# Side products pinned to their written order in TensorE's queue, and the recurrent norm's transposes written later

## The chip, the cores and the metric

The kernel runs on one core of a Trainium2 chip. The metric is the device time of one execution in microseconds, the median of several runs.

## What is computed

One inference step of a four-layer decoder trunk over 320 tokens: a prompt of 256 and eight samples of eight. Layers 0 and 3 are sliding-window attention, layer 1 a gated convolution, layer 2 a gated linear recurrence (HGRN2). Each layer is a norm, an input projection, the mixer with a gate, an output projection and a residual add. Weights are shared by prompt and samples, everything is in float32. Cut to the recurrent layer, which the second part of the change touches:

```python
def hgrn2_mixer(h, w_in, norm_g, w_out, lb, s0):
    proj = h @ w_in
    q, fl, i, z = jnp.split(proj, [C_F_DIM, 2 * C_F_DIM, 2 * C_F_DIM + C_I_DIM], axis=-1)
    f = lbf + (1.0 - lbf) * jax.nn.sigmoid(fl.astype(jnp.float32))
    ...
    o, s_t = gla_chunked(q, k, v, log_f, s0)      # 16 heads of 128 keys and 128 values
    o = rmsnorm(o, norm_g).reshape(bsz, t, C_I_DIM).astype(h.dtype)
    y = (jax.nn.silu(z) * o) @ w_out
    return y, s_t
```

## The kernel before

**Weight products.** All projections run through one loop, `run_step`: 132 steps in all, each 256 output columns. A step has 16 k tiles (128 input features each), a k tile six products: for each of two column halves, weight high part times input high part (L207), times input low part (L208), weight low part times input high part (L209). The split in a high and a low part is made on ScalarE (L171) and, as L172, on VectorE, or on GpSimd for every fourth piece in the steps of `POOL_STEPS` (68 to 85 among them). The first two steps have a loop of their own (`run_first`, L282 to L284).

**Lanes.** Everything else is written as generators in eight lanes. After each k tile `run_step` calls `L.pump()`, which moves each lane on in a fixed order: `evac`, `att0`, `att1`, `smp`, `gpr`, `s0l`, `gla`, `nrm`. `yield n` says that the lane goes on n k tiles later. So the written order of the program is: six weight products, then what the lanes write, then six more. What TensorE does for the lanes is called side products here: scores (L609 to L614), transposes of probabilities (L652), probabilities times values (L674, L676), the samples' attention (L704 to L773), and in the recurrent layer L1085 to L1232.

**Queues.** The written order isn't the queue order. The program goes through a scheduler (`schedule_with_timeline_sim=True`) that fills each engine's queue by a timeline of its own: the earliest written instruction that this timeline has as ready comes next. An instruction whose inputs it has as late is passed by instructions written later. `tc.keep_in_program_order` (the kernel's `pin`) ties an instruction behind the last one written before it on its engine; it ties nothing behind the instruction itself, and makes no engine wait. On TensorE, `run_first` and the token sums L411 are pinned in the kernel before; all other products are free.

**The recurrent layer.** Steps come in pairs of heads: q, f and i columns, then gate columns of an earlier pair. For each head, `gla` writes transposes (L1085 to L1090), scores (L1121, L1122), a state product (L1132, L1134), the output (L1155 to L1158), and two products for the samples' states (L1173). `inter`, in the lane `s0l`, multiplies the samples' queries with their states (L1206, two pairs of two, four k tiles apart) and gathers the result on VectorE (L1211, L1213). With the output, `gla` adds `norm` to its own lane. `norm` writes the inverse root on VectorE (small operations on 128x3, L361 to L369), scales the output (L1223), and after a `yield 4` writes three transposes (L1232) and the copy L1233 to the buffer `on`. The gate (`z_evac`) reads `on`, and its split L420/L421 makes the input of the output projection.

Of the kernel before, what the change touches and what calls it, by code (L numbers as in the profile page):

```python
# [97 lines left out]

NORM_A = ((0, 0),)

Y = {"spt": 7, "spv": 7, "qk": 5, "pt": 9, "pv": 6}


def trunk_kernel(ctx, tc, ins, outs):
    nc = tc.nc
    T, V, A, G, SP = nc.tensor, nc.vector, nc.scalar, nc.gpsimd, nc.sync

    def pool(name, bufs, **kw):
        return ctx.enter_context(tc.tile_pool(name=name, bufs=bufs, **kw))
# [19 lines left out]
    ones = const.tile([128, 128], F, name="ones")  # L129
    pv = const.tile([128, PV_W], F, name="pv")  # L130
# [5 lines left out]
    acc = const.tile([128, NTOK], F, name="acc")  # L136
# [19 lines left out]
    def w_dma(to):  # L156
        while wstate["dma"] < min(to, npieces):
            i = wstate["dma"]
            t = raw.get([128, 4, 256])
            SP.dma_start(out=t, in_=wsrc[i // 4][i % 4].rearrange("p (k c) -> p k c", k=4))  # L160
            rawt[i] = t
            wstate["dma"] += 1

    def w_split(to, pin=lambda i: i):
        while wstate["split"] < min(to, npieces):
            i = wstate["split"]
            t = rawt.pop(i)
            h = whp.get([128, 4, 256], R)
            l = wlp.get([128, 4, 256], R)
            e = G if i % 4 == 0 and i // 4 in POOL_STEPS else V  # L170
            pin(A.activation(out=h, in_=t, func=ACTF.Copy))  # L171
            pin(e.tensor_tensor(out=l, in0=t, in1=h.bitcast(F), op=ALU.subtract))  # L172
            raw.free()
            wht[i], wlt[i] = h, l
            wstate["split"] += 1
# [3 lines left out]
    def run_step(getx, evac):  # L179

        s = step_no[0]
        step_no[0] += 1
        while not mm.ok(2):
            L.pump()
        ps = [mm.get([128, NTOK]) for _ in range(2)]
        final = s == len(wsrc) - 1

        def order(k):

            if final and k >= 12:  # L190
                return [(kk, k // 2 - 6) for kk in range(12 + 2 * (k % 2), 14 + 2 * (k % 2))] if k < 16 else []
            return [(k, 0), (k, 1)]

        for k in range(16):
            i = 4 * s + k // 4
            if k % 4 == 0:
                w_dma(i + 4)
                w_split(i + 3)
                w_dma(i + 7)
            while getx(k) is None:  # L200
                L.pump()
            wh, wl = wht[i], wlt[i]
            for kk, o in order(k):
                a = wh[:, kk % 4, o * 128:(o + 1) * 128]
                b = wl[:, kk % 4, o * 128:(o + 1) * 128]
                xh, xl = getx(kk)
                T.matmul(out=ps[o], lhsT=a, rhs=xh, start=(kk == 0), stop=False)  # L207
                T.matmul(out=ps[o], lhsT=a, rhs=xl, start=False, stop=False)  # L208
                T.matmul(out=ps[o], lhsT=b, rhs=xh, start=False, stop=(kk == 15))  # L209
            if k % 4 == 3:  # L210
                whp.free()
                wlp.free()
                del wht[i], wlt[i]
            L.pump()
        L.add("evac", evac(ps))

    def pin(ins):

        return tc.keep_in_program_order(ins)
# [3 lines left out]
    def run_first():  # L223

        ps = [[mm.get([128, NTOK]) for _ in range(2)] for _ in range(2)]
# [48 lines left out]
        def products(k, steps=(0, 1)):  # L274
            for s in steps:
                for o in range(2):
                    c = slice(o * 128, (o + 1) * 128)
                    if s == 0:
                        a, b = (t[:, k % 4, c] for t in wt[0, k // 4])
                    else:  # L280
                        a, b = (t[:, k % 2, c] for t in wt[1, k // 4, k % 4 // 2])
                    pin(T.matmul(out=ps[s][o], lhsT=a, rhs=hH[k], start=(k == 0), stop=False))  # L282
                    pin(T.matmul(out=ps[s][o], lhsT=a, rhs=hL[k], start=False, stop=False))
                    pin(T.matmul(out=ps[s][o], lhsT=b, rhs=hH[k], start=False, stop=(k == 15)))  # L284
                if s == 0 and k % 4 == 3:
                    whp.free()
                    wlp.free()
                if s == 1 and k % 2:
                    dyn.free(2)
# [24 lines left out]
        for k in range(16):  # L314

            if k % 2 == 0 and k < 14:
                j = k + 2
                split(0, j // 4, j % 4, j % 4 + 2)
                tile_h(j)
                split(1, j // 4, j % 4, j % 4 + 2)  # L320
                tile_h(j + 1)
                if j % 4 == 2 and j < 8:
                    load(0, j // 4 + 2, 0, 4)
                    load(1, j // 4 + 2, 0, 4)
                squares(k // 2)
            if k < 14:
                products(k)
        SP.dma_start(out=scv, in_=ins["scv"])

        products(14, (0,))  # L330
        products(15, (0,))
        step_no[0] = 2
        wstate["dma"] = wstate["split"] = 8
# [21 lines left out]
    def wait(p, n=1):  # L355
        while not p.ok(n):
            yield 1

    def rsqrt(x, out, t, scratch_engine=None):

        V.tensor_scalar(out=out.bitcast(I32), in0=x.bitcast(I32), scalar1=1, scalar2=None,  # L361
                        op0=ALU.arith_shift_right)
        V.tensor_scalar(out=out.bitcast(I32), in0=out.bitcast(I32), scalar1=-1, scalar2=0x5F3759DF,
                        op0=ALU.mult, op1=ALU.add)
        V.tensor_scalar(out=x, in0=x, scalar1=-0.5, scalar2=None, op0=ALU.mult)
        for _ in range(3):
            V.tensor_tensor(out=t, in0=out, in1=out, op=ALU.mult)  # L367
            V.tensor_tensor(out=t, in0=t, in1=x, op=ALU.mult)
            V.scalar_tensor_tensor(out=out, in0=t, scalar=1.5, in1=out, op0=ALU.add, op1=ALU.mult)  # L369

    hH, hL = {}, {}
# [33 lines left out]
    def r_job(ticks=3):  # L405
        yield ticks
        yield from wait(sm)
        yield from wait(wk, 2)
        ps = sm.get([128, NTOK])

        pin(T.matmul(out=ps, lhsT=ones, rhs=acc, start=True, stop=True))  # L411
        ms, t = wk.get([128, NTOK]), wk.get([128, NTOK])
        V.tensor_scalar(out=ms, in0=ps, scalar1=1.0 / D, scalar2=EPS, op0=ALU.mult, op1=ALU.add)
        sm.free()
        rsqrt(ms, rb, t)
        wk.free(2)
# [69 lines left out]
    def layer_a(li):  # L486
# [108 lines left out]
        def att_unit(pr, gp, qd, ql):  # L595
            while not (kdone[0] and vdone[0]):
                yield 1
            yield Y["qk"]
            P = {}
# [41 lines left out]
            dyn.free(3)  # L641
            yield Y["pt"]
            parts = {}
            for kv in range(2):
# [3 lines left out]
                for o in range(2):  # L648
# [13 lines left out]
                    yield 1  # L662
            yield Y["pv"]
            yield from wait(xo)
# [23 lines left out]
        def smp_job(pr):  # L688
            while not (kdone[0] and vdone[0]):
                yield 1  # L690
            for hb in range(2):
# [22 lines left out]
                for b2 in range(2):  # L714
# [34 lines left out]
                    tiny.free(3)  # L749
                    yield Y["spt"]  # L750
                    while not (sm.ok(2) and wk.ok(3)):
# [15 lines left out]
                    sm.free(2)  # L767
                    yield Y["spv"]
                    yield from wait(sm)
# [49 lines left out]
        if li == 0:  # L819
            L.add("evac", k_evac(first[0]))  # L820
            L.add("evac", v_evac(first[1]))
        else:
            run_step(get_h, k_evac)
            run_step(get_h, v_evac)
        for pr in range(2):
            for gp in range(4):
                run_step(get_h, q_evac(pr, gp))
# [102 lines left out]
    def layer_c(li):  # L930
# [287 lines left out]
        def norm(h, o, ss):  # L1218
            r, t = tiny.get([128, 3]), tiny.get([128, 3])
            V.tensor_scalar(out=ss, in0=ss, scalar1=1.0 / 128, scalar2=EPS, op0=ALU.mult, op1=ALU.add)  # L1220
            rsqrt(ss, r, t)
            for i in range(3):
                V.tensor_scalar(out=o[:, i, :], in0=o[:, i, :], scalar1=r[:, i:i + 1], scalar2=None, op0=ALU.mult)  # L1223
            tiny.free(3)
            yield 4
            yield from wait(sm)
            if h % 2 == 0:
                yield from wait(xo)
                on[h // 2] = xo.get([128, 2, NTOK])
            pt = sm.get([128, 384])  # L1230
            for i in range(3):
                T.transpose(out=pt[:, i * 128:(i + 1) * 128], in_=o[:, i, :], identity=ident)  # L1232
            A.activation(out=on[h // 2][:, h % 2, :], in_=pt[:, 0:NTOK], func=ACTF.Copy)  # L1233
            sm.free()
            wk.free()
            done.add(h)
# [56 lines left out]
    ps = [sm.get([128, 1]) for _ in sizes]  # L1293
# [7 lines left out]
    for i, (c, n) in enumerate(sizes):  # L1301
        T.matmul(out=pr[:, c:c + n], lhsT=r[0:n, i:i + 1].to_broadcast([n, 128]), rhs=ident[0:n, 0:n], start=True,
                 stop=True)
    for p in range(8):
        for o in (0, 1) if p == 0 else (slice(0, 2),):
            o = slice(o, o + 1) if p == 0 else o
# [133 lines left out]
```

## Time and profile before

| | |
|---|---|
| time, median of 3 runs (lowest, highest) | 2092.29 us (2089.16, 2093.36) |
| profiled execution: time, span | 2096.16 us, 2094.3 us |
| mean granted TensorE clock in it | 0.991 |
| TensorE, VectorE, ScalarE, GpSimd busy | 98%, 68%, 48%, 31% of the span |

The span is that of the profiled execution, from its first to its last instruction; its time has some 2 us around it. Busy time of TensorE is time in which at least one product is under way; products overlap, so the mean time of one is longer than the distance between two starts. The clock is the share of full speed that was granted to TensorE.

### The profile page before, as it was taken

How to read it: one execution, taken by the hardware profiler on the slowest of the kernel's cores; microseconds unless marked ns; L12 is line 12 of the kernel's file. 1: busy time of each engine (PE TensorE's matmuls, PEld its weight loads, DVE VectorE, ACT ScalarE, POOL GpSimd, SP SyncE). 2: the span in 40 equal slices, each digit the busy share in tenths (PEclk: the TensorE clock that was granted, in tenths of full speed). 3: DMA queues.
4: the chain of work that ended last, by engine and by line, in shares of the span. 5: the costliest groups of instructions: out<-in, count | busy, mean ns of one | idle time of the engine just before them, and what ended most of it. 6: DMA issues, size and time to landing. Idle time of an engine off the chain costs nothing.

```text
span 2094.3 us, 36939 instructions
## 1 busy us (share of the span) xinstructions
PE 2051.8 (98%) x13994; PEld 2034.8 (97%) x13994; DVE 1421.2 (68%) x2748; ACT 1008.9 (48%) x2027; POOL 655.1 (31%) x1002
## 2 busy tenths in 40 slices
PE   8989999999999999999999999999999999999997
PEld 8989999999999999999998999999999999999997
DVE  7888865564455455455777998888875677876644
ACT  6567753433333333344454544454544357775442
POOL 0576400110000000012555565345401146752010
PEclk9999999999999999999999999999999999999998
DMA  6433565444444444455454454444465544445542
GB/s 240 129 121 121 181 187 173 151 151 151 150 147 149 150 151 151 154 169 170 145 163 137 161 164 143 163 154 153 145 222 175 170 148 142 127 137 174 166 151 101
DMA packets 106442, 326.45 MB, mean 156 GB/s; under 512 B 16600, under 2 KB 25304, under 8 KB 106264
## 3 DMA queue, kind: packets, MB, share of 16 engines
q1 hardware_dynamic: 105400, 322.75, 47.8%
q8 instruction: 110, 1.80, 0.4%
q10 hardware_dynamic: 864, 1.34, 0.2%
q14 instruction: 68, 0.56, 0.1%
HBM read 301.88 MB, written 22.17 MB: 155 GB/s over the span
## 4 chain that ended last, share of the span: by engine, by line
PE 86%; DVE 7%; ACT 1%; issue 1%; POOL 1%; DMA 0%; DVEq 0%; POOLq 0%; ACTq 0%
PE mm L208 26%; PE mm L209 26%; PE mm L207 26%; DVE wlp L172 1%; PE sm L652 1%; PE sm L674 1%; DVE bg L1176 1%; PE sm L1206 1%; DVE tiny L369 1%; DVE wk L1014 0%; DVE dyn L421 0%; PE sm L1122 0%; PE sm L614 0%; DVE tiny L367 0%; ACT whp L171 0%
## 5 line engine op out<-in xcount | busy, mean ns | idle before, releaser
L207 PE MATMUL mm<-hp,whp 128*128 128x320 f32 x3136 | 976.6, 312 | 2.4 <-DVE wk L428 2.4
L208 PE MATMUL mm<-hp,whp 128*128 128x320 f32 x3136 | 976.5, 311 | 0.0
L209 PE MATMUL mm<-hp,wlp 128*128 128x320 f32 x3136 | 974.3, 311 | 1.2 <-DVE wlp L172 1.2
L171 ACT ACTIVATE whp<-raw 128x1024 fp32r<-128x1024 f32 x520 | 550.4, 1059 | 802.0 <-PE mm L208 660.9
L172 DVE TENSOR_TENSOR wlp<-raw,whp 128x1024 fp32r<-128x1024 f32 x477 | 602.6, 1264 | 466.7 <-ACT whp L171 460.9
L207 PEld LDWEIGHTS mm<-hp,whp 128*128 128x128 f32 x3136 | 590.8, 188 | 4.0 <-DVE wk L428 2.8
L209 PEld LDWEIGHTS mm<-hp,wlp 128*128 128x128 f32 x3136 | 590.4, 188 | 3.5 <-DVE wlp L172 2.2
L208 PEld LDWEIGHTS mm<-hp,whp 128*128 128x128 f32 x3136 | 590.8, 188 | 2.3
L208 PE MATMUL mm<-dyn,whp 128*128 128x320 f32 x1024 | 316.5, 309 | 0.0
L207 PE MATMUL mm<-dyn,whp 128*128 128x320 f32 x1024 | 316.4, 309 | 0.0
L209 PE MATMUL mm<-dyn,wlp 128*128 128x320 f32 x1024 | 316.4, 309 | 0.0
L402 POOL TENSOR_TENSOR acc<-acc,wk 128x320 f32<-128x320 f32 x58 | 62.0, 1070 | 446.8 <-ACT wk L401 444.7
L209 PEld LDWEIGHTS mm<-dyn,wlp 128*128 128x128 f32 x1024 | 192.2, 188 | 0.0
L208 PEld LDWEIGHTS mm<-dyn,whp 128*128 128x128 f32 x1024 | 192.2, 188 | 0.0
L207 PEld LDWEIGHTS mm<-dyn,whp 128*128 128x128 f32 x1024 | 192.2, 188 | 0.0
L172 POOL TENSOR_TENSOR wlp<-raw,whp 128x1024 fp32r<-128x1024 f32 x43 | 105.4, 2451 | 139.2 <-ACT whp L171 134.1
L637 POOL TENSOR_SCALAR wk<-wk,tiny 128x256 f32<-128x256 f32 (+1 forms) x96 | 96.9, 1023 | 25.1 <-ACT bg L778 6.9
L885 POOL COPY wk<-wk 128x2 f32<-128x2 f32 x16 | 2.9, 184 | 296.8 <-DVE wk L875 296.8
L626 ACT ACTIVATE wk<-wk,tiny 128x128 f32<-128x128 f32 (+1 forms) x128 | 56.7, 444 | 21.0 <-DVE tiny L620 20.7
L1203 POOL TENSOR_TENSOR dyn<-bg,dyn 128x512 fp32r<-128x512 f32 x32 | 50.8, 1613 | 44.2 <-ACT dyn L1202 44.2
L1112 POOL TENSOR_TENSOR xo<-xo,lcp 128x512 fp32r<-128x512 f32 x32 | 34.2, 1074 | 82.3 <-DVE xo L1105 80.6
L428 DVE TENSOR_TENSOR wk<-mm,rb 128x320 f32<-128x320 f32 x112 | 50.8, 484 | 12.5 <-PE mm L209 11.8
(268 smaller groups left out, 2284.8 us busy)
## 6 DMA issues: line engine op xcount, KB each, us to landing
raw<-in_a_w_in_dram SPq DMA_DIRECT2D x142, 512.0 KB, 3.6
raw<-in_b_w_in_dram SPq DMA_DIRECT2D x128, 512.0 KB, 3.5
raw<-in_c_w_in_dram SPq DMA_DIRECT2D x128, 512.0 KB, 3.5
raw<-in_a_w_out_dram SPq DMA_DIRECT2D x64, 512.0 KB, 3.5
raw<-in_b_w_out_dram SPq DMA_DIRECT2D x32, 512.0 KB, 3.4
raw<-in_c_w_out_dram SPq DMA_DIRECT2D x32, 512.0 KB, 3.5
bg<-in_s_dram SPq DMA_DIRECT2D x16, 512.0 KB, 4.5
out_hgrn_s_dram<-bg SPq DMA_DIRECT2D x16, 512.0 KB, 2.7
```

Of the source, the lines that this page charges most:

```text
L171: pin(A.activation(out=h, in_=t, func=ACTF.Copy))
L172: pin(e.tensor_tensor(out=l, in0=t, in1=h.bitcast(F), op=ALU.subtract))
L207: T.matmul(out=ps[o], lhsT=a, rhs=xh, start=(kk == 0), stop=False)
L208: T.matmul(out=ps[o], lhsT=a, rhs=xl, start=False, stop=False)
L209: T.matmul(out=ps[o], lhsT=b, rhs=xh, start=False, stop=(kk == 15))
L369: V.scalar_tensor_tensor(out=out, in0=t, scalar=1.5, in1=out, op0=ALU.add, op1=ALU.mult)
L402: G.tensor_tensor(out=acc, in0=acc, in1=t, op=ALU.add)
L428: V.tensor_tensor(out=w[o][:, 0:NTOK], in0=ps[o], in1=rb, op=ALU.mult)
L626: A.activation(out=p[:, c], in_=p[:, c], func=ACTF.Exp, scale=-1.0, bias=mx[:, kv, blk:blk + 1], accum_out=sums[:, kv, blk:blk + 1])
L637: G.tensor_scalar(out=p[:, c], in0=p[:, c], scalar1=sums[:, kv, blk:blk + 1], scalar2=None, op0=ALU.mult)
L1112: G.tensor_tensor(out=t, in0=kv[:, u, 1, :].bitcast(F).unsqueeze(1).to_broadcast([128, 4, 128]), in1=umask[:, 4 * u:4 * u + 4].unsqueeze(2 ...
L1203: G.tensor_tensor(out=sl, in0=src, in1=sh.bitcast(F), op=ALU.subtract)
```

## The change

`T`, by which all products were called, becomes a class whose `matmul` and `transpose` pin each product behind what was written before it on TensorE. The weight products of `run_step` are called through `M`, the plain engine, and stay free. The products that were pinned by hand are pinned by the class. In `norm`, the pause before the transposes goes from 4 to 10 k tiles.

```diff
-Y = {"spt": 7, "spv": 7, "qk": 5, "pt": 9, "pv": 6}
+Y = {"spt": 7, "spv": 7, "qk": 5, "pt": 9, "pv": 6, "nrm": 10}
...
-    T, V, A, G, SP = nc.tensor, nc.vector, nc.scalar, nc.gpsimd, nc.sync
+    M, V, A, G, SP = nc.tensor, nc.vector, nc.scalar, nc.gpsimd, nc.sync
+
+    class T:
+        @staticmethod
+        def matmul(**kw):
+            return tc.keep_in_program_order(M.matmul(**kw))
+
+        @staticmethod
+        def transpose(**kw):
+            return tc.keep_in_program_order(M.transpose(**kw))
...
-                T.matmul(out=ps[o], lhsT=a, rhs=xh, start=(kk == 0), stop=False)
+                M.matmul(out=ps[o], lhsT=a, rhs=xh, start=(kk == 0), stop=False)
...
-                    pin(T.matmul(out=ps[s][o], lhsT=a, rhs=hH[k], start=(k == 0), stop=False))
+                    T.matmul(out=ps[s][o], lhsT=a, rhs=hH[k], start=(k == 0), stop=False)
...
-        pin(T.matmul(out=ps, lhsT=ones, rhs=acc, start=True, stop=True))
+        T.matmul(out=ps, lhsT=ones, rhs=acc, start=True, stop=True)
...
             tiny.free(3)
-            yield 4
+            yield Y["nrm"]
             yield from wait(sm)
```

## Rows read from the trace of the kernel before

**Rows 1.** The page's busy time (us, share of the span) of TensorE and VectorE.

```profile
PE 2051.8 (98%) x13994; PEld 2034.8 (97%) x13994; DVE 1421.2 (68%) x2748; ACT 1008.9 (48%) x2027; POOL 655.1 (31%) x1002
```

**Rows 2.** Groups by line, TensorE, 1640 to 1660 us: count | busy us, mean ns.

```profile
L207 PE MATMUL mm<-dyn,whp 128*128 128x320 f32 x46 | 14.2, 309 | 0.0
```

**Rows 3.** Who waited for whom, TensorE: us in total, times, longest.

```profile
PE sm L1232 <- DVE wk L1223: 10.7, 7, 3.7
PE sm L755 <- DVE wk L747: 5.8, 1, 5.8
...
PE sm L609 <- DVE dyn L586: 3.2, 2, 1.8
```

**Rows 4.** Windows: us, busy time and count by engine, then granted TensorE clock (PEclk).

```profile
300.00:400.00 100.00, 100.00 (x684) 100.00 (x683) 59.06 (x75) 42.72 (x61) 9.33 (x9) 1.00 0.53 168
...
71.50:74.90 3.40, 3.40 (x14) 3.21 (x14) 2.49 (x3) 0.11 (x1) 0.54 (x1) 0.50 0.55 171
146.60:153.40 6.80, 5.91 (x22) 5.28 (x23) 5.82 (x16) 3.11 (x8) 4.21 (x8) 0.50 0.01 5
1109.20:1115.90 6.70, 4.59 (x15) 3.75 (x16) 3.81 (x8) 0.44 (x1) 6.62 (x21) 0.50 0.45 146
1259.40:1262.70 3.30, 3.30 (x14) 3.24 (x15) 1.46 (x3) 1.40 (x3) 0.00 (x0) 0.50 0.52 166
```

**Rows 5.** Groups by line, TensorE, from a layer's first product to its L411.

```profile
L207 PE MATMUL mm<-hp,whp 128*128 128x320 f32 x16 | 4.9, 309 | 0.0
```

**Rows 6.** Between L1206's pairs of head 8 (groups), and L1206 of head 10 (timeline).

```profile
L208 PE MATMUL mm<-hp,whp 128*128 128x320 f32 x8 | 2.5, 309 | 0.0
...
1369.01 1.09 PE L1206 MATMUL sm<-dyn,qzs 128*128 128x512 f32 x4
```

**Rows 7.** Timeline, TensorE: start us, us, line, operation.

```profile
71.61 0.74 PE L612 MATMUL sm<-bg,dyn 128*128 128x512 f32 x1
...
74.23 0.31 PE L611 MATMUL sm<-bg,dyn 128*128 128x128 f32 x1
```

**Rows 8.** Groups by line, VectorE and ScalarE, whole span.

```profile
L1176 DVE SCALAR_TENSOR_TENSOR bg<-bg,tiny,sm 128x128 f32<-128x128 f32 x128 | 35.4, 340 | 5.1 <-PE sm L1173 5.0
...
L1233 ACT ACTIVATE xo<-sm 128x320 f32<-128x320 f32 x16 | 6.9, 431 | 23.6 <-PE sm L1232 23.6
```

**Rows 9.** Groups by line, TensorE, L1155 to L1232: head 13, then head 7.

```profile
L207 PE MATMUL mm<-hp,whp 128*128 128x320 f32 x24 | 7.4, 309 | 0.0
...
L207 PE MATMUL mm<-hp,whp 128*128 128x320 f32 x19 | 5.9, 309 | 0.0
```

**Rows 10.** Timeline at head 6, VectorE and GpSimd; groups of VectorE, 1380 to 1420.

```profile
1255.53 2.17 DVE L369 SCALAR_TENSOR_TENSOR tiny<-tiny,tiny 128x3 f32<-128x3 f32 x1
...
1255.28 2.40 POOL L172 TENSOR_TENSOR wlp<-raw,whp 128x1024 fp32r<-128x1024 f32 x1
...
L369 DVE SCALAR_TENSOR_TENSOR tiny<-tiny,tiny 128x3 f32<-128x3 f32 x6 | 0.9, 158 | 0.1
```

**Rows 11.** Timeline, TensorE: L1232 of heads 1, 6 and 10 [idle before].

```profile
1110.99 0.45 PE L1232 MATMUL sm<-ident,wk 128*128 128x128 f32 x1 [3.69 <-DVE wk L1223]
...
1259.39 0.69 PE L1232 MATMUL sm<-ident,wk 128*128 128x128 f32 x2 [2.04 <-DVE wk L1223]
...
1398.78 0.33 PE L1232 MATMUL sm<-ident,wk 128*128 128x128 f32 x1 [0.20 <-DVE wk L1223]
```

**Rows 12.** Timeline at the recurrent layer's end: ScalarE, VectorE, TensorE.

```profile
1552.18 0.44 ACT L1233 ACTIVATE xo<-sm 128x320 f32<-128x320 f32 x1 [1.04 <-PE sm L1232]
...
1555.44 0.89 DVE L421 TENSOR_TENSOR dyn<-wk,dyn 128x320 fp32r<-128x320 f32 x2
...
1561.95 0.31 PE L207 MATMUL mm<-dyn,whp 128*128 128x320 f32 x1
```

**Rows 13.** Timeline at head 12: the norm's L1223 (VectorE) and L1232 (TensorE).

```profile
1464.14 0.68 DVE L1223 TENSOR_SCALAR wk<-wk,tiny 128x128 f32<-128x128 f32 x3
...
1465.16 0.27 PE L1232 MATMUL sm<-ident,wk 128*128 128x128 f32 x1
```

More of the change, by code (lines that the diff above doesn't have):

```diff
@@ L206, in run_step @@
                 xh, xl = getx(kk)
-                T.matmul(out=ps[o], lhsT=a, rhs=xh, start=(kk == 0), stop=False)
-                T.matmul(out=ps[o], lhsT=a, rhs=xl, start=False, stop=False)
-                T.matmul(out=ps[o], lhsT=b, rhs=xh, start=False, stop=(kk == 15))
+                M.matmul(out=ps[o], lhsT=a, rhs=xh, start=(kk == 0), stop=False)
+                M.matmul(out=ps[o], lhsT=a, rhs=xl, start=False, stop=False)
+                M.matmul(out=ps[o], lhsT=b, rhs=xh, start=False, stop=(kk == 15))
             if k % 4 == 3:
@@ L281, in products @@
                         a, b = (t[:, k % 2, c] for t in wt[1, k // 4, k % 4 // 2])
-                    pin(T.matmul(out=ps[s][o], lhsT=a, rhs=hH[k], start=(k == 0), stop=False))
-                    pin(T.matmul(out=ps[s][o], lhsT=a, rhs=hL[k], start=False, stop=False))
-                    pin(T.matmul(out=ps[s][o], lhsT=b, rhs=hH[k], start=False, stop=(k == 15)))
+                    T.matmul(out=ps[s][o], lhsT=a, rhs=hH[k], start=(k == 0), stop=False)
+                    T.matmul(out=ps[s][o], lhsT=a, rhs=hL[k], start=False, stop=False)
+                    T.matmul(out=ps[s][o], lhsT=b, rhs=hH[k], start=False, stop=(k == 15))
                 if s == 0 and k % 4 == 3:
```

## The prediction

> **What bounds the kernel now.** I read the busy shares of the page first: TensorE is busy for 98% of the span, VectorE for 68% [rows 1]. The kernel therefore ends when TensorE's queue ends, and only two things shorten it: less work in that queue, or less waiting. Then the groups by line for TensorE. Nearly all of it is the 12480 weight products; in a stretch that holds nothing else, 46 of each of their three lines, 138 in all, pass in 20 us, so one takes about 145 ns from start to start, and a k tile of six of them 0.87 us [rows 2]. The change alters neither their number nor their operands, nor those of the side products (transposes, scores, probabilities times values, the recurrence).
>
> What is left is waiting, so the table of TensorE's waits came next [rows 3]. The norm transposes L1232 wait 10.7 us in 7 waits, the sample transposes L755 5.8 us once, the scores L609 3.2 us in two. The other rows are the start, the final norm and a few hand-overs of 1 to 2 us that no edit touches. Last the windows behind the longest waits, for TensorE's clock: behind three of the L1232 waits, behind L755 and behind L609 the granted clock is 0.50, the lower of its two levels, after the engine had stood idle for 1.8 to 5.8 us; in a long stretch without waits it is at the full level [rows 4]. So a wait costs itself and some products at half speed.
>
> What the L1232 waits could give back at most: 10.7 us of idle time, and half of the busy time in the three half-clock windows behind them, 4.59 us at head 1 and 3.30 us at each of heads 6 and 8 (one is shown): 11.19 / 2 = 5.6 us. Together 16.3 us, 0.8% of the time.
>
> **The change, part by part.**
>
> *The pin on side products.* It adds no instruction and no semaphore; it only says that a side product isn't queued ahead of the last TensorE instruction written before it. The weight products lose their only pins in the first two steps to the same class, so those stay pinned, and all later ones stay free. A free weight product written later can therefore still pass a pinned side product whose input is late. The kernel before has such a case: L411, pinned already, is written 24 products into the next layer (three k tiles and the one before its lane is pumped), and in the trace 46 of that layer's products (16 of L207, 15 each of the other two lines) stand ahead of it [rows 5]. So the pin is a floor, not a place, and it moves only those side products that the queue now has ahead of their place, or in another order than two side products were written in.
>
> Ahead of their place: L1206, the state products of the recurrent layer, written in two pairs four k tiles apart. For head 8 the trace has the pairs 24 products apart (8 of each line), as written; for head 10 all four stand in one row [rows 6], and heads 12 and 14 look the same, with one more single product at the layer's start. Those 13 instructions go back by up to 26 products, 26 x 0.145 = 3.8 us later. Bounds: nothing gained, since no idle time is counted before L1206; lost, at most that 3.8 us if its readers had no slack. Their result is first needed by products written eight k tiles on (48 products, 7.0 us), so 3.8 us is hidden by 7.0 us of weight products. I take 0; if that cover were gone, the price is rival 2.
>
> In another order: in the attention layers L612 and L614 of the first key head now run before the second key head's L611 when that one's input is late, as at 71 us: L612 at 71.61, the late L611 at 74.23 [rows 7]. They are written after it, so pinned they wait for it, 2.6 us here; by my count of the queue a dozen of the 32 groups are like this and none moves by more than 70 products (10 us). TensorE loses nothing, as weight products fill in. VectorE gets some score reductions (L620, 0.35 to 0.48 us each) later, but has other work of that layer. In the recurrent layer's first heads two L1173 are likewise held behind late L1157; four L1176 updates of 0.28 us (35.4 / 128) then fall behind the norm instead of ahead of it [rows 8], which could bring L1232 of those two heads forward by 1.1 us each. Bounds for all of this: a gain of 2.2 us, a loss of the same if the order turns the other way. I take 0 to -1 us.
>
> *The transposes, 10 k tiles instead of 4.* What moves is three transposes, the copy L1233 (0.43 us on ScalarE, [rows 8]) and the claim of one output buffer. It issues no DMA, and no DMA queue is passed. The question is whether six k tiles (36 products, 5.2 us) of written place move them in the queue at all. The norm is written together with L1155, so the written place is 24 products behind L1155 before and 60 after. In the trace, head 13 has 70 products between L1155 and its first L1232 (24 of L207, 23 each of the others), head 7 has 56 (19, 19 and 18) [rows 9]; counting all sixteen heads the same way, head 7 is the smallest, thirteen have 69 to 90, and heads 1 and 3, two of those that wait, have 135 and 143. The transposes already stand where the scheduler took the norm to be finished, beyond the new written place in 15 of 16 heads. Moving a floor that lies below them moves nothing; head 7, which has no wait, moves by 4 products (0.6 us). The waits come from elsewhere: the norm's small VectorE operations run later than planned. At head 6 one L369 takes 2.17 us, beside a GpSimd split L172 of 2.40 us that starts at 1255.28 just ahead of it; around head 10, after the last step that gives GpSimd a split, six of them take 0.158 us on average [rows 10]. The transposes then wait 2.04 us [rows 11]. Neither edit changes that meeting, so the waits stay. I take 0 for this edit, with bounds of -16.3 us (above) and +0.6 us.
>
> The Trainium skill ("SBUF — State Buffer", Who interferes with whom) says that a VectorE instruction with two SBUF inputs and a GpSimd instruction that reads SBUF exclude each other for the whole of whichever starts first. The rows of head 6 agree with it. By that rule, heads from 10 on, where no split runs on GpSimd, couldn't get such a wait, and rival 2 would cost nothing; by the rows alone it keeps its price.
>
> What is held longer: the norm's work buffer and the copy's turn on ScalarE, six k tiles in written order. At the layer's end the last head's copy runs at 1552.18, its last split L421 ends at 1556.33, and TensorE first reads it at 1561.95 [rows 12]: 5.6 us of slack against 5.2 us even if the transposes did move by all 36 products. So that end costs nothing either way, but only just.
>
> *Sum.* 0 (L1206) + 0 to -1 (order) + 0 (transposes) = 0 to -1 us. The profiled execution took 2096.16 us (span 2094.3 us), 3.9 us above the median of the runs, 2092.29; I apply the difference to the median: 2091.3 to 2092.3, and forecast 2091.5 us.
>
> **Rivals.**
>
> *1. The written place does decide.* If pinned side products keep their place against later weight products too, the transposes go 36 products (5.2 us) behind, past every late norm: the waits of head 1 (3.69 us) and of heads 6 and 8 (2.04 us) all fit in. All of it gone gives 2092.3 - 16.3 = 2076.0 us. For: six of the seven waits are under 2.1 us. Against: L411 and the counts above.
>
> *2. Later state products make three heads wait (slower).* Heads 6 and 8 have L1206 as written, and their transposes wait 2.04 us; head 10 has L1206 early and waits 0.20 us, heads 12 and 14 don't wait [rows 11]. If the change gives heads 10, 12 and 14 the order of 6 and 8, each costs 2.04 us and half of 3.30 us of work at the lower clock, 3.7 us; three make 11.1 us: 2103.4 us. It decides once the norm ends more than its present lead later: head 12's L1223 ends at 1464.82 and its transpose starts at 1465.16 [rows 13], so 0.3 us is enough there. Against: by the kernel's list of steps, GpSimd takes no split after step 85, and these heads' norms come later.
>
> *3. The first layer's new order takes L755's wait away.* 5.8 us and half of 5.91 us of work at the lower clock [rows 4], 8.8 us: 2083.5 us. For: the wait is one place where VectorE is behind plan, and L612 and L614 are reordered just ahead of it. Against: what VectorE is late by isn't made less by another order, and may only show elsewhere.
>
> **How the numbers follow.** Chances: forecast 0.42 (its own range 2086 to 2098, since a queue that is reordered anywhere shifts waits of 2 us at places nobody names), rival 1 0.25, rival 2 0.23, rival 3 0.10. A change of 0.2%, 4.2 us, is about what a measurement of this kernel tells from none. Faster by more: 0.25 + 0.10 + 0.05 of the forecast's own spread = 0.40; slower by more: 0.23 + 0.05 = 0.28; the rest, 0.32, is within. The range runs from rival 1 to rival 2, 2076 to 2104; full or excess versions of either are left out, some 0.2.
>
> **What the profile after would show.** Right: L1232 of heads 1, 3, 6 and 8 still waits for L1223, about 10 us in all, with 70 and more products between L1155 and L1232; L1206 of heads 10, 12 and 14 in two pairs 24 products apart; L612 never ahead of its group's second L611; half clock behind the same waits. Wrong: no L1232 in TensorE's table of waits (rival 1), L1232 waits of 2 us at heads 10, 12 and 14 (rival 2), no L755 wait near 147 us (rival 3). It would also be wrong if TensorE waited for new releasers in the first layer, through score reductions that come later than VectorE has other work for.

## The result, and the profile after

The changed kernel takes 2080.46 us (median of 4 runs, 2079.55 to 2080.64), the kernel before 2091.91 us in the same comparison: ratio 0.9944, 95% interval 0.9932 to 0.9957. It is 11.4 us faster. The time lies in the range of the prediction, but not at its forecast of 2091.5 us, which was no change.

In the rows of the kernels with pins, pinned products have the line of the class, L113 (matmul) or L117 (transpose), and the tiles tell which they are. Other lines are some 11 or 12 higher than before: the split L172 is L184, the norm's L1223 is L1234, L369 is L381, L620 is L631.

TensorE's waits after (us in total, times, longest), to set beside [rows 3]:

```profile
PE sm L117 <- DVE wk L1234: 5.8, 5, 2.0
...
PE sm L117 <- DVE wk L758: 3.6, 1, 3.6
...
PE sm L113 <- DVE dyn L597: 1.8, 1, 1.8
```

The norm transposes wait 5.8 us where they waited 10.7, the sample transposes 3.6 where they waited 5.8, the scores 1.8 where they waited 3.7 in all (a wait of 1.6 us for a split is new), and the 2.4 us of the last layer's evacuation, too small a row to be among [rows 3], are gone. All rows of that table together make 22.1 us after and 32.4 before: 10.3 us less idle time.

The windows behind the waits (the last numbers are the granted clock, the DMA share and GB/s), beside [rows 4]:

```profile
71.50:74.90 3.40, 3.40 (x24) 3.31 (x25) 3.37 (x6) 0.46 (x2) 0.73 (x2) 1.00 0.52 160
142.80:149.60 6.80, 5.70 (x22) 5.24 (x23) 5.84 (x19) 2.21 (x6) 3.80 (x6) 0.50 0.26 77
1103.00:1109.80 6.80, 6.60 (x44) 6.39 (x45) 3.79 (x7) 3.49 (x5) 4.80 (x5) 1.00 0.41 142
1248.90:1252.20 3.30, 3.30 (x15) 3.30 (x15) 2.93 (x5) 2.27 (x6) 0.00 (x0) 0.50 0.36 118
1317.10:1320.40 3.30, 3.30 (x16) 3.25 (x16) 1.15 (x2) 1.72 (x4) 0.00 (x0) 0.50 0.59 182
```

Of five stretches at the lower level three are left, with 12.3 us of busy time where there were 20.5. Half of the difference is 4.1 us. With the idle time that makes 14.4 of the 15.6 us between the two profiled spans (2094.3 and 2078.7 us). The profiled execution of before was some 4 us above the median of its runs, which is why the medians differ by 11.4 us only.

Not all of the 14.4 us is the change's. e8_pin_l1206 (below) has no pin in the attention layers, and in its trace too the window from 71.50 to 74.90 us is at the full level, with 23 products (14 in the kernel before), and the scores wait 2.4 us. So the gain at the first scores can come without the pins, from one execution to the next.

The parts of the queue that the prediction named: between L1206's pairs of head 10 (groups by line, TensorE, 1357.1 to 1360.5 us; L220 and L221 have 8 each too):

```profile
L219 PE MATMUL mm<-hp,whp 128*128 128x320 f32 x8 | 2.5, 309 | 0.0
```

And head 6's transposes (timeline, TensorE):

```profile
1248.31 1.05 PE L117 MATMUL sm<-ident,wk 128*128 128x128 f32 x5 [1.86 <-DVE wk L1234]
```

L1206 went back to its written place, 24 products apart, as predicted [rows 6]. Head 6's transposes still wait, 1.86 us where it was 2.04 [rows 11], and head 8's 2.03 us; head 1's wait went from 3.69 to 0.86 us.

### The profile page after: what moved, and what is told of

Read it like the earlier page. It is cut to its first block, busy times and chain, and to the rows that moved or that the text cites. A ratio compares the mean times of both kernels' runs of the same rounds, so it can differ in the third digit from the quotient of the medians.

```text
span 2078.7 us, 36968 instructions
## 1 busy us (share of the span) xinstructions
PE 2046.8 (98%) x13994; PEld 2031.6 (98%) x13994; DVE 1406.0 (68%) x2748; ACT 1008.3 (49%) x2027; POOL 669.7 (32%) x1002
## 4 chain that ended last, share of the span: by engine, by line
PE 89%; DVE 6%; POOL 1%; ACT 0%; issue 0%; DVEq 0%; POOLq 0%; ACTq 0%
PE mm L221 27%; PE mm L219 27%; PE mm L220 27%; PE sm L113 6%; PE sm L117 2%; DVE wlp L184 1%; DVE bg L1187 1%; DVE wk L1025 0%; DVE tiny L380 0%; DVE tiny L379 0%; DVE tiny L375 0%; DVE tiny L381 0%; DVE xo L1318 0%; DVE dyn L432 0%; ACT whp L183 0%
## 5 line engine op out<-in xcount | busy, mean ns | idle before, releaser
L221 PE MATMUL mm<-hp,wlp 128*128 128x320 f32 x3136 | 974.1, 311 | 1.6 <-POOL wlp L184 1.6
L220 PE MATMUL mm<-hp,whp 128*128 128x320 f32 x3136 | 974.9, 311 | 0.0
L184 DVE TENSOR_TENSOR wlp<-raw,whp 128x1024 fp32r<-128x1024 f32 x477 | 601.8, 1263 | 473.3 <-ACT whp L183 472.3
L221 PEld LDWEIGHTS mm<-hp,wlp 128*128 128x128 f32 x3136 | 589.6, 188 | 3.1 <-POOL wlp L184 1.8
L220 PEld LDWEIGHTS mm<-hp,whp 128*128 128x128 f32 x3136 | 590.2, 188 | 1.9
L221 PE MATMUL mm<-dyn,wlp 128*128 128x320 f32 x1024 | 316.7, 309 | 0.0
L220 PE MATMUL mm<-dyn,whp 128*128 128x320 f32 x1024 | 316.6, 309 | 0.0
L221 PEld LDWEIGHTS mm<-dyn,wlp 128*128 128x128 f32 x1024 | 192.2, 188 | 0.0
L220 PEld LDWEIGHTS mm<-dyn,whp 128*128 128x128 f32 x1024 | 192.2, 188 | 0.0
L184 POOL TENSOR_TENSOR wlp<-raw,whp 128x1024 fp32r<-128x1024 f32 x43 | 105.5, 2454 | 140.5 <-ACT whp L183 122.7
L648 POOL TENSOR_SCALAR wk<-wk,tiny 128x256 f32<-128x256 f32 (+1 forms) x96 | 104.9, 1106 | 37.0 <-DVE tiny L641 24.8
L117 PE MATMUL sm<-ident,wk 128*128 128x128 f32 (+1 forms) x376 | 65.6, 282 | 9.4 <-DVE wk L1234 5.8
L631 DVE CUSTOM_DVE_ANT_0 wk<-sm,lcp,nsink 128x128 f32<-128x128 f32 (+1 forms) x128 | 46.2, 413 | 22.2 <-PE sm L113 21.9
L117 PEld LDWEIGHTS sm<-ident,wk 128*128 128x128 f32 (+1 forms) x376 | 48.5, 142 | 12.8 <-DVE wk L1234 6.0
```

What stands on the lines that cost most here:

```text
L117: return tc.keep_in_program_order(M.transpose(**kw))
L220: M.matmul(out=ps[o], lhsT=a, rhs=xl, start=False, stop=False)
L221: M.matmul(out=ps[o], lhsT=b, rhs=xh, start=False, stop=(kk == 15))
L631: V.tensor_tensor_reduce(out=p[:, c], in0=S[kv][blk], in1=maskp[:, c], scale=1.0, scalar=nsink[:, 32 * j + h:32 * j + h + 1], op0=ALU.add, ...
L648: G.tensor_scalar(out=p[:, c], in0=p[:, c], scalar1=sums[:, kv, blk:blk + 1], scalar2=None, op0=ALU.mult)
```

## The experiments

Each was compared with the kernel before on the same chip. A ratio is to that kernel.

### The two parts apart: e1_pause, e2_pins

```diff
 e1_pause: kernel before      e2_pins: kernel after
-            yield 4          -..., "nrm": 10}
+            yield 10         +..., "nrm": 4}
```

> The kernel before with the pause of 10 k tiles alone, no product newly pinned. Theory A (the pins reorder the queue and with it VectorE's order; the pause is a floor that lies below the transposes' place): 0, within 4 us of the kernel before, and L1232 still waits some 10 us. Theory B (the written place decides, so the pause makes the gain in the recurrent layer): about 8 us faster, since by the two traces the kernel after gains 8 us of its lead in that layer, and L1232's waits halve.

> The kernel after with the pause put back to 4 k tiles: all pins, no longer pause. Theory A: all of the gain, 11 us faster than before, with L1232 waiting some 6 us as in the kernel after. Theory B: only what the attention layers give, 4 to 7 us faster than before, and L1232 waits 10 us.

The pause alone: 2091.93 us, ratio 1.0003 (0.9995 to 1.0012). The pins alone: 2081.52 us, 0.9954 (0.9941 to 0.9966), against 0.9944 for both. So the pins make nearly all of the gain and the pause alone makes none. Theory A holds for the times. Of the norm transposes' waits in e2_pins it expected 6 us, and they are 8.3 us in 7. With the pins, the pause may give the rest, 1 us, which these intervals don't separate from 0.

```profile
PE sm L1232 <- DVE wk L1223: 9.2, 6, 2.6
```

That is e1_pause's row in the table of waits. It isn't quite as before (10.7 us in 7), and the transposes' places didn't stay: counted in the queue, 12 of 48 stand up to 38 products earlier, and head 7's three stand 4 later, which the prediction had. A changed written order of L1232 and L1233 changes the scheduler's timeline for other operations too.

### Which layer: e3_pins_attn, e4_pins_rec

The pins as in e2_pins, but in one of the two kinds of layer the side products are called through `M`:

```diff
 e3_pins_attn, in layer_c     e4_pins_rec, in layer_a
-T.transpose(...)             -T.matmul(...)
+M.transpose(...)             +M.matmul(...)
```

> The pins on the attention layers' side products alone, pause 4. Both theories: the lead that the kernel after has outside the recurrent layer, 4.5 us in the first layer and 3 us in the last, so 5 to 7.5 us faster than before; the recurrent layer as before, with L1232 waiting some 10 us. If the two attention layers give nothing alone, the gain is all in the recurrent layer and both theories are short.

> The pins on the recurrent layer's side products alone, pause 4. Theory A: 4 to 8 us faster than before, from fewer or shorter L1232 waits at heads 1 to 4, with L755's 5.8 us as before. Theory B: 0, within 4 us, since without the pause the transposes stand where they stood.

The attention layers' pins: 2083.26 us, 0.9965 (0.9953 to 0.9978), 8 us faster. The recurrent layer's: 2088.62 us, 0.9989 (0.9981 to 0.9998), 3 us faster, less than theory A's 4 to 8 and within theory B's 4. The sum is what both give together. The larger part comes from the layers in which the prediction had counted on nothing.

### Which pin in attention: e5_pin_l612, e6_pins_other

```diff
 e5_pin_l612: the only pin on a lane's product but L411; e6_pins_other: this one and the other scores free, the rest of layer_a pinned
-                M.matmul(out=Sb, lhsT=ql[:, o, 128:256], rhs=kb[:, pr, :, :], start=True, stop=False)
+                T.matmul(out=Sb, lhsT=ql[:, o, 128:256], rhs=kb[:, pr, :, :], start=True, stop=False)
```

> Of all pins only the one on the second scores' first product (L612, written behind the second key head's L611) in the attention layers; pause 4. Theory A1 (the gain in attention comes from scores kept in written order, so that all products of a group run together): the same 8 us as with all attention pins, 2083 us, and the L755 wait at 3.6 us. Theory A2 (any other order of the first layer's queue would do as well or as badly: the waits fall where they happen to): a time between 2080 and 2095 us, with waits at other places.

> The pins on all side products of the attention layers but the scores (transposes, probabilities times values, the samples' products); pause 4. Theory A1: no gain, within 4 us of the kernel before, L755 waits 5.8 us as before. Theory A2: again a time between 2080 and 2095 us with waits at other places, a gain as likely as a loss.

One pin, on L612, gives as much as the whole change: 2079.66 us, 0.9948 (0.9935 to 0.9960), more than the 8 us expected. The other attention pins: 2087.89 us, 0.9984 (0.9975 to 0.9993), 2.7 us faster. (The class also pins the first two steps, L411 and the final norm's products in both; e8_pin_l1206 has these pins too and gains nothing.) Two rows of TensorE's timeline in e5_pin_l612, and one of its table of waits, show how:

```profile
72.85 0.22 PE L622 MATMUL sm<-bg,dyn 128*128 128x128 f32 x1
72.91 0.44 PE L113 MATMUL sm<-bg,dyn 128*128 128x512 f32 x1
```

```profile
PE sm L766 <- DVE wk L758: 1.1, 1, 1.1
```

The second scores' first product (L113 here) now stands right behind the second L611 (L622 here); before, it ran 2.6 us ahead of it [rows 7]. The sample transposes wait 1.1 us instead of 5.8. Windows from 60 to 200 us, first of e8_pin_l1206, which has no pin on this layer's products, and then of e5_pin_l612, tell what that is worth:

```profile
60.00:200.00 140.00, 130.78 (x899) 127.49 (x898) 114.84 (x328) 96.74 (x289) 95.28 (x120) 0.98 0.39 129
```

```profile
60.00:200.00 140.00, 135.47 (x944) 132.63 (x943) 117.17 (x345) 102.69 (x310) 101.93 (x123) 1.00 0.42 133
```

TensorE starts 45 products more with the pin, some 6.5 us at 0.145 us each, in single executions. e6_pins_other has 898, so its 2.7 us don't come from here. VectorE's table of waits between 60 and 200 us, first of the kernel before and then of e5_pin_l612, has one row that falls with that wait:

```profile
DVE dyn L658 <- ACT dyn L657: 5.9, 6, 2.1
```

```profile
DVE dyn L669 <- ACT dyn L668: 1.3, 3, 0.5
```

These are the splits of the transposed probabilities. VectorE stood 5.9 us in six waits before them, 1.3 us in three with the pin; e6_pins_other still has 5.9 us, and L755's wait of 5.8. But its waits for the scores (L620 for L611, L631 for L622) grew from 7.4 to 11.3 us, so these rows alone don't explain the sample transposes' shorter wait, and in e3_pins_attn the splits wait 1.3 us too while those transposes wait 3.6. What is shown is the end of it: VectorE comes to L744, from which L747 and then the sample transposes follow, at 146.46 us in the kernel before, at 144.81 in e8_pin_l1206 and at 140.28 in e5_pin_l612. So a TensorE order that costs TensorE nothing brought VectorE's work for the samples forward, and TensorE got the time back some 70 us later, at the sample transposes. By which operations it did so wasn't followed. Theory A2 isn't out by this for the last layer: there the 2.4 us of waits behind the evacuation are gone in e5_pin_l612 and e6_pins_other alike, with different orders.

### Which pin in the recurrent layer: e7_pin_l1173, e8_pin_l1206

```diff
 e7_pin_l1173                                 e8_pin_l1206
-M.matmul(out=sp, lhsT=kv[:, u, 0, :], ...    -M.matmul(out=ps, lhsT=qz[:, u, :], ...
+T.matmul(out=sp, lhsT=kv[:, u, 0, :], ...    +T.matmul(out=ps, lhsT=qz[:, u, :], ...
```

> Only the products L1173 pinned behind the outputs L1157 and L1158; pause 4. The prediction's order term: the four state updates L1176 (0.28 us each) fall behind the norm at heads 1 and 3, whose waits of 3.7 and 1.9 us get shorter by 1.1 us each: 0 to 2.2 us faster than before, most of the 2.8 us that all recurrent pins gave. Rival: the recurrent pins' gain is another pin's (L1121, L1122): no change, waits of 3.7 and 1.9 us as before.

> Only the state products L1206 pinned, so that those of heads 10, 12 and 14 go back to their written place, 26 products later; pause 4. The prediction's sum: 0, within 2 us of the kernel before. Its rival 2: 11 us slower, L1232 waiting 2 us at heads 10, 12 and 14.

L1206 alone: 2092.35 us, 1.0004 (0.9995 to 1.0013). No change, as the sum had it, and no new waits at heads 10 to 14; rival 2 is out. L1173 alone: 2087.55 us, 0.9981 (0.9973 to 0.9990), as much as all pins of that layer and some 3 us where 0 to 2.2 were expected. But not by what I had expected. VectorE's timeline at head 1 in e7_pin_l1173 (the state updates, the norm's first operation, its last):

```profile
1094.90 2.15 DVE L1187 SCALAR_TENSOR_TENSOR bg<-bg,tiny,sm 128x128 f32<-128x128 f32 x8
1096.96 0.16 DVE L1231 TENSOR_SCALAR tiny<-tiny 128x3 f32<-128x3 f32 x1
...
1104.44 0.68 DVE L1234 TENSOR_SCALAR wk<-wk,tiny 128x128 f32<-128x128 f32 x3
```

The eight updates do run later, but still ahead of the norm, not behind it. Other work of VectorE changed places with them, and the norm starts 7.0 us before TensorE reaches the transposes (at 1104.01) where it was 4.5 us in the kernel before (L1220 at 1102.82, TensorE there at 1107.30). Head 1's wait falls from 3.69 to 0.86 us, and head 3's of 1.90 us is gone. Head 4's goes from 0.5 to 0.6 us, and a new one of 1.1 us comes at head 5.

### The written place set behind the norm: e10_pause24, e13_pause24_only

The change with a pause of 24 k tiles, and the kernel before with that pause and no pin.

```diff
 e10_pause24: kernel after     e13_pause24_only: kernel before
-..., "nrm": 10}               -            yield 4
+..., "nrm": 24}               +            yield 24
```

> The kernel after with a pause of 24 k tiles instead of 10, so that the transposes' written place lies behind the place where they stand now (12 of 16 heads stood less than 14 k tiles, 84 products, behind it). Floor theory: now the written place decides, L1232's waits (5.8 us in the kernel after) go below 1 us, and with the half clock behind them 6 to 9 us are gained: 2072 to 2075 us, unless the last heads' output comes too late for the output projection, where 12 us of later transposes stand against 5.6 us of slack: then a new wait of some 5 us there and 2077 to 2080 us. Rival: the waits come from VectorE being late as a whole and only move to other side products: 2080 us as the kernel after.

> The kernel before with a pause of 24 k tiles and no new pin. Floor theory: the written place now lies behind the place where the norm is ready in nearly all heads, so L1232's waits (10.7 us) go below 1 us; as in the run with all pins and this pause, up to 6 us of waits at other side products of heads 1 to 5 take their place: 5 to 10 us faster than before, 2081 to 2086 us, and heads 6 to 10 without any wait. Rival (waits only move): 0.

Without pins: 2080.82 us, 0.9950 (0.9937 to 0.9964), 10 us faster, just under what I expected. With all pins: 2076.69 us, 0.9929 (0.9915 to 0.9942), between the floor theory's 2072 to 2075 and the rival's 2080. L1232 isn't in either table of waits any more. Other products of the first heads wait instead, for VectorE's L1116 (3.0 us in three) and L1224 (1.7 us once) above all in e10_pause24.

In e10_pause24 they make 6 us, about what L1232 waited in the kernel after, and no stretch of the recurrent layer is at the lower clock there. The time is 3.8 us below the kernel after's, but the intervals of the two ratios overlap, so this gain isn't clear of noise. In e13_pause24_only they make 3.9 us against 11.9 us of the kernel before. No wait shows at the layer's end.

### Two splits taken from GpSimd: e12_splits

```diff
-POOL_STEPS = set(range(3, 14)) | set(range(68, 86)) | set(range(108, 122))
+POOL_STEPS = set(range(3, 14)) | set(range(68, 86)) - {81, 85} | set(range(108, 122))
```

> The kernel after with the split L172 (L184 there) of steps 81 and 85 moved from GpSimd to VectorE, the two that stand beside the norm's small operations of heads 6 and 8. Lock theory: L369 (L381 there) beside it takes 0.2 instead of 2.2 us, and the waits of heads 6 and 8 (1.86 and 2.03 us) go below 0.5 us; VectorE pays 1.2 us twice, inside its idle time: 2076 to 2079 us. Rival: VectorE is late by its own 1.2 us in place of the 2 us, waits of about 1 us stay: 2079 to 2081 us.

2072.93 us, 0.9912 (0.9899 to 0.9926): 7.5 us faster than the kernel after (6.7 by the ratios), more than expected. The two groups below are timelines at head 6, first of the kernel after (GpSimd, VectorE), then of e12_splits (VectorE, then TensorE's transposes, now without a wait):

```profile
1243.16 2.41 POOL L184 TENSOR_TENSOR wlp<-raw,whp 128x1024 fp32r<-128x1024 f32 x1
...
1243.40 2.19 DVE L375 TENSOR_SCALAR tiny<-tiny 128x3 int32<-128x3 int32 x1
```

```profile
1242.68 0.15 DVE L375 TENSOR_SCALAR tiny<-tiny 128x3 int32<-128x3 int32 x1
...
1248.06 1.03 PE L117 MATMUL sm<-ident,wk 128*128 128x128 f32 x8
```

The operation beside the split, here L375 and not L381, took 2.19 us, and 0.15 us without it. The waits of heads 6 and 8 are gone but for 0.13 us. They were 3.9 us, and half of the two windows of 3.30 us behind them, which are at the full level here, is 3.3 us more: 7.2 us, about the gain. That isn't the lock alone: with the split on VectorE the scheduler also put those transposes 17 and 7 products later (2.5 and 1.0 us), so how much each did stays open.

### The parts that gave most: e11_l612_pause24

The one pin on L612 and the pause of 24, nothing else.

> The pin on L612 in the attention layers and the pause of 24, nothing else. If the layers are independent, the sum of the two parts measured alone: L612's 10.9 us and what the pause of 24 gives alone, 5 to 10 us: 2070 to 2075 us, faster than the kernel after by 5 to 10 us. If the recurrent pins are needed as well: 2077 us or more.

2069.82 us, 0.9898 (0.9884 to 0.9911): the fastest version, 21 us faster than before. The parts add up, 0.9948 times 0.9950 is 0.9898, so the recurrent pins aren't needed. No stretch between the start and the final norm is at the lower clock.

## Why the prediction was right or wrong

**The bound** was right: TensorE's queue sets the time, and what changed is its idle time and what ran at the lower clock behind it. Nearly all of the difference between the two profiles is accounted for by these two terms.

**The signs** that were named for the profile after came only in part. L1232 waits 5.8 us in all, not about 10, and one of the stretches at the lower clock behind it is gone.

**The pin is a floor** was right in what it does to TensorE's queue, and L1206 costs nothing was right (e8_pin_l1206).

**The step that failed** is "In another order", which I took as 0 to -1 us with bounds of 2.2 us either way. It measured -10.9 us for L612 alone (e5_pin_l612) and -8 us for all attention pins (e3_pins_attn). I had priced what the new order does to TensorE and written that VectorE "has other work of that layer", as if that made it neutral. But all the waits in question are waits for VectorE, so VectorE's order is what sets them. My bounds came from the one reader that I could name (four L1176 updates), not from the waits that VectorE's lateness makes, 10.7, 5.8, 3.2 and 2.4 us. That the total still lay in the range is luck: rival 1's price, for a mechanism that gave nothing here (e1_pause), set the range's lower end. Rival 3 had the place (the sample transposes L755, 8.8 us) and got 0.10. In the changed kernel it came true in part, since they still wait 3.6 us; with L612's pin alone they wait 1.1 us, for some 6.5 us of gain in that layer. The argument against it, that lateness may only show elsewhere, fell with that run: the time of the whole kernel is 10.9 us shorter.

**The transposes' pause** was right in its size, 0 (e1_pause), and in its reason for the most part: the waits of heads 6 and 8 stayed in the kernel after. That "nothing moves" was too much said: 15 transposes moved in e1_pause, and with the pins L1232's waits are 8.3 us without the longer pause (e2_pins) and 5.8 with it. Rival 1 fell at 10 k tiles. What it would have brought, transposes behind every late norm, comes without any pin once the floor lies above their place (e13_pause24_only, -10 us).

**The updates behind the norm** had the right heads (1 and 3) and a gain of the right order, by a way that didn't happen (e7_pin_l1173).

**The slack at the layer's end** is enough: even with 24 k tiles no wait shows there.

**The shared lock** of VectorE and GpSimd as the source of the waits of heads 6 and 8 is supported by e12_splits, not isolated. That heads from 10 on can't get such a wait was wrong. The rule that the prediction cites from the Trainium skill ("SBUF — State Buffer", Who interferes with whom) is for every GpSimd instruction that reads SBUF, not for the weight splits alone. The trace of the kernel before agrees: at head 10 GpSimd works on the states (L1203), and small operations of the norm take over 1 us beside it (timelines of GpSimd and VectorE):

```profile
1389.25 6.23 POOL L1203 TENSOR_TENSOR dyn<-bg,dyn 128x512 fp32r<-128x512 f32 x4 [9.33 <-ACT dyn L1202]
```

```profile
1393.01 1.25 DVE L367 TENSOR_TENSOR tiny<-tiny 128x3 f32<-128x3 f32 x1
```

The 0.158 us of [rows 10] is L369's mean alone, and head 10's transposes do wait, 0.20 us [rows 11]. Rival 2 is out by e8_pin_l1206, not by that rule.

**Open:** why each group of VectorE operations comes out where it does, and by which of them L755's wait fell. The orders are the scheduler's, and one order's merit over another was measured, not derived.

## What to carry to other kernels

Where one engine's in-order queue is full and all its waits are for a second engine, an edit to the first engine's order is to be costed by what it does to the second one's order: bound it by the waits that are there, not by the operations that it moves. A pin or a later written place in a reordering scheduler is only a floor, and here it gave nothing until it lay above where the scheduler puts the instruction; measure that distance in the queue first. Try the pins one at a time, since one of them can carry the whole gain and leave room for a better version.

## What the runs showed of the hardware

Some small VectorE operations take as long as the GpSimd operation beside them, also some with a single source: at 1274.71 us one of L365 takes 2.53 us beside a GpSimd split of 2.44 us. One line of the kernel before, 128x3 elements (count, shortest/median/longest ns):

```profile
L365 DVE TENSOR_SCALAR tiny<-tiny x17: 153/158/2526, 1066.0 to 2080.7; 128x3 f32<-128x3 f32 x17
```

Counted over L361 to L369 at that size in the same trace: 62 of 204 overlap a GpSimd operation in time, and 20 of those 62 take over 0.6 us; of the other 142 none does.

The same wait doesn't always cost the same clock. Head 6's transposes wait 2.04 us both in the kernel before and in e3_pins_attn; behind it the clock is at the lower level before [rows 4], and at the full level in e3_pins_attn (timeline, then window):

```profile
1254.73 0.33 PE L1243 MATMUL sm<-ident,wk 128*128 128x128 f32 x1 [2.04 <-DVE wk L1234]
```

```profile
1254.80:1258.10 3.30, 3.30 (x25) 3.24 (x26) 1.90 (x5) 2.36 (x5) 0.00 (x0) 1.00 0.57 170
```

In 3.30 us TensorE starts 25 products there, and 14 in the kernel before. So a single profiled execution misprices the clock's share of a wait by some microseconds in this kernel, either way.
